# One split of V per chunk, low parts placed over the moving rows of U, expert choices looked up among 16 per side, and more gather pairs issued beside the routing

## The chip, the cores and the metric

The kernel runs on one core of one Trainium2 chip. The time is device microseconds of one execution, the median of several runs; the profiles show one execution each. Engines are called as in the profile: PE (TensorE matmul) and PEld (its weight loads), DVE (VectorE), ACT (ScalarE), POOL (GpSimd), SP (SyncE, which here only issues DMAs).

## What is computed

The program is one forward pass over 512 tokens of width 1024: a first block (neighbourhood attention beside a recurrent mixer, then a PEER feed-forward part), and a second block of two ordinary layers. The change touches the PEER part alone. Cut to that:

```python
def peer_ffn(h, wq, sub_keys, u, v):        # h 512 x 1024, u and v 16384 x 1024
    def block(t):                            # 128 tokens at a time
        q = (t @ wq).reshape(128, 8, 2, 128)
        s = jnp.einsum('tpcd,pckd->tpck', q, sub_keys)
        s1, i1 = lax.top_k(s[:, :, 0], 16)   # best 16 of 128 keys, each side
        s2, i2 = lax.top_k(s[:, :, 1], 16)
        cand = (s1[..., :, None] + s2[..., None, :]).reshape(128, 8, 256)
        cidx = (i1[..., :, None] * 128 + i2[..., None, :]).reshape(128, 8, 256)
        top, pos = lax.top_k(cand, 16)       # best 16 of the 256 sums
        idx = jnp.take_along_axis(cidx, pos, axis=-1)
        g = jax.nn.softmax(top, axis=-1)
        a = jax.nn.gelu(jnp.einsum('tpkd,td->tpk', u[idx], t), approximate=False)
        return jnp.einsum('tpk,tpkd->td', g * a, v[idx])
```

Each token has 8 heads with 16 chosen experts: 128 rows of u and 128 rows of v per token.

## The kernel before

All products are in fp32, made of three matmuls of a reduced-precision fp32 type: each operand is split into a high part (a copy by ACT) and a low part (operand minus high part, by DVE), and high x high, high x low and low x high are added up in PSUM.

**PEER, two ways at once.** Token tile 0 (128 tokens) goes by *gathers*: for each of its 128 (head, rank) places an indirect DMA on POOL's queue fetches 128 rows of U (one for each token, 512 KB), and DVE takes the dot product with the token (L1161, tile `gr`); later an indirect DMA fetches the rows of V, and DVE adds them weighted to `accg` (L1166). That is 256 gathers in 128 pairs (`gathered`, L1130). Five buffers `gr` form a ring, and a gather is issued four places ahead of the DVE operation that consumes it. Token tiles 1 to 3 (384 tokens) go *densely*: all 16384 experts are computed in 128 chunks of 128, and a weight table W with zeros for the experts that a token has not chosen is multiplied in.

**The U stage.** `ahead` (L1368) runs over the 128 chunks. `rows_u` loads 512 KB of U and splits it (`wh` on ACT L1349, `wl` on DVE L1350); `hidden` makes 24 matmuls of 128x384 and a gelu, and the result `act` goes to DRAM (`Ad`). Beside it `route` works through the tiles: `topk` (DVE alone) finds the experts of a tile, and `spread` turns them into the table W by one-hot matmuls: for each group of four tokens DVE makes `oh` and `go` (L1321), ACT scales `go`, PE multiplies, ACT copies the bank, and W goes to DRAM (`Wd`). The list `GATHER` gives for each of five phases (phase t runs topk of tile t beside spread of tile t-1) what a gather pair costs in the planner `weave`, which always takes the next piece of the generator that has spent least; a smaller number issues pairs more often. `PACE` (2.66) is the price of a chunk there. PE's order is the written one. The ring of gathers starts in phase 1, after the choices of tile 0 are known.

**The V stage.** After the last chunk of U, `operands` (L1377) prepares one chunk of V: it loads `act` and V, multiplies `act` by the weights `Wr` (L1390), and splits V and act. The split of V is written twice: `vh` (L1391, ACT) and `vl` (L1393, DVE), and again in the last line by the helper `split` (L134 on ACT, L136 on DVE); only the second pair is used. `products` makes 18 matmuls of 128x512 per chunk, four chunks behind. The gathers that are left are spread evenly over the first 120 chunks. The order on PE, DVE and ACT is the written one. The pools on the right side of SBUF are a stack: `h2` (the moving rows of U, the tokens) is closed after the last chunk of U, and `pm` (act, Wr, vh, vl, sh, sl) is opened in its place.

**The tail.** The six PSUM banks and `accg` are scaled by a row `gt2r`, added to X, normed (L1084 to L1104), and the second block begins. Line numbers from L1054 on are one to twelve different in the changed kernel; the order fences below show both.

Of the kernel before, what the change touches and what calls it, by code (L numbers as in the profile page):

```python
# [22 lines left out]
TD = S - T0  # L23
# [5 lines left out]
VBUFS = 6  # L29
# [2 lines left out]
WT = 16  # L32
GBUFS = 5
GAHEAD = 4
GATHER = (13.0, 13.0, 9.0, 6.0, 4.5)
OPS_LAG = 4
TAIL = 2
STATE = 3.0
# [54 lines left out]
class Net:  # L93
# [931 lines left out]
    def peer(self):  # L1025
        nc, p = self.nc, self.p
# [15 lines left out]
        pq = self.pool("pq", "right")  # L1042
# [9 lines left out]
        run(ahead)  # L1052
        self.shut("pa")
        self.shut("h2")  # L1054
        pm = self.pool("pm", "right")
        ar = self.pool("ar")
        for i in range(GROUP - WLATE):
            self.spread_rows(pm, 0, i)
        rows = self.rows_of(3, "gt2r", ar)
        banks = [[self.bank() for _ in range(2)] for _ in range(3)]  # L1060
        ops = {}
        held = []
# [2 lines left out]
        E = mybir.EngineType  # L1065
        with self.tc.manual_schedule(engines={E.PE, E.DVE, E.Activation}):
            for e in range(128 + OPS_LAG):
# [6 lines left out]
                if e >= OPS_LAG:  # L1074
                    x = e - OPS_LAG
                    if x < 128 - TAIL:
                        self.products(banks, range(3), [(x, ops.pop(x))])
                    else:
                        held.append((x, ops.pop(x)))
        run(gather)  # L1080
        for t in range(3):
            self.products(banks, [t], held)
        self.shut("pm")
# [160 lines left out]
    def topk(self, pq, sc, io):  # L1244
        nc = self.nc
        m1 = pq.tile([128, 8, 2, 16], F32, name="m1")
        i1 = pq.tile([128, 8, 2, 16], U32, name="i1")
        for h in range(8):
            for c in range(2):
                tmp = pq.tile([128, 128], F32, name="tmp", bufs=2)  # L1250
                self.top16(m1[:, h, c], i1[:, h, c], sc[:, h * 2 + c], tmp)
                yield 1.0
        f1 = pq.tile([128, 8, 2, 16], F32, name="f1")
        nc.vector.tensor_copy(f1, i1)
        nc.vector.tensor_scalar(f1[:, :, 0], f1[:, :, 0], 128.0, None, op0=OP.mult)
        cand = pq.tile([128, 8, 50], F32, name="cand")
        cidx = pq.tile([128, 8, 50], F32, name="cidx")
        for dst, src in ((cand, m1), (cidx, f1)):
            o = 0
            for a in range(8):  # L1260
                n = 16 // (a + 1)
                nc.vector.tensor_tensor(out=dst[:, :, o:o + n], in0=src[:, :, 0, a:a + 1].to_broadcast([128, 8, n]),
                                        in1=src[:, :, 1, :n], op=OP.add)
                o += n
            nc.vector.tensor_tensor(out=dst[:, :, o:], in0=src[:, :, 0, 8:],
                                    in1=src[:, :, 1, 0:1].to_broadcast([128, 8, 8]), op=OP.add)
        yield 2.7
        top = pq.tile([128, 8, 16], F32, name="top")
        pos = pq.tile([128, 8, 16], U32, name="pos")
        for h in range(8):  # L1270
            tmp = pq.tile([128, 128], F32, name="tmp", bufs=2)
            self.top16(top[:, h], pos[:, h], cand[:, h], tmp[:, :50])
            yield 0.6
        pf = pq.tile([128, 8, 16], F32, name="pf")
        nc.vector.tensor_copy(pf, pos)
        idx = pq.tile([128, 128], F32, name="idx", bufs=2)
        for h in range(8):
            eq = pq.tile([128, 16, 50], F32, name="eq")
            nc.vector.tensor_tensor(out=eq, in0=io[:, None, :50].to_broadcast([128, 16, 50]),
                                    in1=pf[:, h].unsqueeze(2).to_broadcast([128, 16, 50]), op=OP.is_equal)  # L1280
            self.anchor = nc.vector.tensor_tensor(out=eq, in0=eq, in1=cidx[:, h:h + 1].to_broadcast([128, 16, 50]), op=OP.mult)
            nc.vector.tensor_reduce(idx[:, h * 16:(h + 1) * 16], eq, axis=AX.X, op=OP.add)
            yield 2.7
        ii = pq.tile([128, 128], I32, name="ii")
        nc.vector.tensor_copy(ii, idx)
        e1 = pq.tile([128, 128], F32, name="e1", bufs=2)
        e2 = pq.tile([128, 128], F32, name="e2", bufs=2)
        it = pq.tile([128, 128], I32, name="it", bufs=2)
        nc.vector.tensor_scalar(it, ii, 7, None, op0=OP.logical_shift_right)
        nc.vector.tensor_copy(e1, it)  # L1290
        it = pq.tile([128, 128], I32, name="it", bufs=2)
        nc.vector.tensor_scalar(it, ii, 127, None, op0=OP.bitwise_and)
        nc.vector.tensor_copy(e2, it)
# [8 lines left out]
        return e1, e2, g.rearrange("p h k -> p (h k)")  # L1302

    def spread(self, pq, t, e1, e2, g, io):

# [71 lines left out]
    def operands(self, pm, e):  # L1377

        nc, p = self.nc, self.p
        n, j = divmod(e, GROUP)  # L1380
        if j == 0:
            self.Wr = self.Wn
        a = pm.tile([128, TD], F32, name="act", bufs=ABUFS)
        nc.sync.dma_start(a, self.Ad[e])
        v = self.st.tile([128, 2, 512], F32, name="w", bufs=WBUFS)
        nc.sync.dma_start(v.rearrange("p a b -> p (a b)"), p['V'][e])
        vh, vl = (pm.tile([128, 2, 512], FR, name=n, bufs=VBUFS) for n in ("vh", "vl"))
        sh, sl = (pm.tile([128, TD], FR, name=n, bufs=VBUFS) for n in ("sh", "sl"))
# [472 lines left out]
```

## Time and profile before

| | us |
|---|---|
| median of 3 runs | 3129.43 |
| lowest and highest run | 3128.04, 3133.86 |
| the profiled execution | 3129.33 |
| its span | 3127.5 |

| engine | busy us | share | 
|---|---|---|
| PE | 2937.5 | 94% |
| PEld | 2488.1 | 80% |
| DVE | 2033.6 | 65% |
| ACT | 1387.3 | 44% |
| POOL | 458.0 | 15% |

The span is one program of many stages; a share over the whole of it says little about any of them. The stages of this case are told apart by time: the U stage from 678.27 (its first matmul) to 1338.12 (the start of its last), and the V stage from 1349.76 to 1986.64. Busy time of PE is modelled, and matmuls overlap in the records: the distance between starts is the price of one, not its length. The same holds for DVE, where an operation's record is about 0.08 us longer than the distance to the next start.

### The profile page before, as it was taken

The numbers are of one execution on the slowest core, as the hardware profiler recorded it, in microseconds if no ns is written. First come the engines' busy times: TensorE is split into PE (matmuls) and PEld (weight loads), VectorE is DVE, ScalarE is ACT, GpSimd is POOL, SyncE is SP. The second block draws the span as 40 slices with busy tenths as digits, with TensorE's granted clock in tenths as the row PEclk, the third lists the DMA queues.
The fourth block names the chain that finished last, engine by engine and source line by source line (L and its number), as shares of the span: only waits on it lengthen the run. The fifth ranks groups of instructions, "written<-read, shape, count | busy, mean of one in ns | idle before, by whom it ended". The sixth has DMA issues, their size and how long they took to land.

```text
span 3127.5 us, 42558 instructions
## 1 busy us (share of the span) xinstructions
PE 2937.5 (94%) x16010; PEld 2488.1 (80%) x16010; DVE 2033.6 (65%) x3768; ACT 1387.3 (44%) x2404; POOL 458.0 (15%) x399
## 2 busy tenths in 40 slices
PE   7898998999999999978888888899999999999998
PEld 5787987899998999966666666678888887788887
DVE  5744496459999867679999999644433335543323
ACT  4233563343466667844444444533322234433222
POOL 2100000000111222224444443000000000000000
PEclk9999999999999999999999999899999999999999
DMA  6622202345666778899999998222333222123332
GB/s 251 226 69 78 62 1 95 108 133 193 225 231 218 267 263 290 294 311 337 342 338 337 341 341 306 87 71 90 101 99 97 95 88 66 51 88 96 100 102 81
DMA packets 262510, 544.63 MB, mean 174 GB/s; under 512 B 21904, under 2 KB 139936, under 8 KB 257952
## 3 DMA queue, kind: packets, MB, share of 16 engines
q1 hardware_dynamic: 200096, 350.28, 34.1%
q0 software_dynamic: 36896, 134.25, 12.6%
q10 hardware_dynamic: 25312, 57.39, 5.0%
q8 instruction: 125, 2.05, 0.3%
q14 instruction: 81, 0.66, 0.1%
HBM read 489.38 MB, written 52.45 MB: 173 GB/s over the span
## 4 chain that ended last, share of the span: by engine, by line
PE 53%; DVE 23%; issue 10%; DMA 2%; POOL 1%; ACT 1%; SPq 0%; POOLq 0%; ACTq 0%; DVEq 0%
PE bank L123 51%; DVE vl L1393 4%; DVE accg L1166 3%; DVE gr L1161 3%; DVE act L1390 2%; DVE sl L1394 2%; DVE wl L1350 1%; POOL gr L1142 1%; PE bank L608 1%; PE bank L1500 1%; DVE A L826 1%; DVE KX L802 1%; DVE QX L803 0%; DMA gr<-in_Un_dram,iu 0%; DVE tmp L1240 0%
## 5 line engine op out<-in xcount | busy, mean ns | idle before, releaser
L123 PE MATMUL bank<-hh,wl 128*128 128x512 f32 (+2 forms) x2304 | 837.0, 364 | 31.7 <-DVE wl L1350 21.2
L123 PE MATMUL bank<-hh,wh 128*128 128x512 f32 (+2 forms) x2304 | 840.5, 366 | 10.8 <-ACT wh L149 4.4
L123 PE MATMUL bank<-hl,wh 128*128 128x512 f32 (+2 forms) x2304 | 834.8, 362 | 1.8 <-DVE hl L273 1.1
L150 DVE TENSOR_TENSOR wl<-w,wh 128x1024 fp32r<-128x1024 f32 (+2 forms) x280 | 295.2, 1055 | 645.9 <-ACT wh L149 639.0
L149 ACT ACTIVATE wh<-w 128x1024 fp32r<-128x1024 f32 (+2 forms) x280 | 257.4, 920 | 746.1 <-PE bank L123 602.9
L123 PEld LDWEIGHTS bank<-hh,wl 128*128 128x128 f32 x2304 | 437.8, 190 | 89.9 <-DVE wl L1350 32.3
L123 PEld LDWEIGHTS bank<-hh,wh 128*128 128x128 f32 x2304 | 436.7, 190 | 64.8 <-ACT wh L149 5.0
L123 PEld LDWEIGHTS bank<-hl,wh 128*128 128x128 f32 x2304 | 437.8, 190 | 49.2 <-DVE hl L273 1.9
L1142 POOL DMA_INDIRECT gr<-in_V_dram,iv x128 | 212.4, 1660 | 588.1 <-DVE gr L1161 546.2
L123 PE MATMUL bank<-vl,sh 128*128 128x512 f32 x768 | 247.7, 404 | 42.9 <-DVE vl L136 42.8
L123 PE MATMUL bank<-vh,sh 128*128 128x512 f32 x768 | 245.4, 401 | 36.9 <-ACT vh L134 36.9
L123 PE MATMUL bank<-vh,sl 128*128 128x512 f32 x768 | 237.9, 391 | 0.0
L123 PEld LDWEIGHTS bank<-vl,sh 128*128 128x128 f32 x768 | 137.6, 188 | 105.7 <-DVE vl L136 82.0
L123 PEld LDWEIGHTS bank<-vh,sh 128*128 128x128 f32 x768 | 139.6, 188 | 89.8 <-ACT vh L134 63.5
L1142 POOL DMA_INDIRECT gr<-in_Un_dram,iu x128 | 165.9, 1296 | 295.1 <-DVE gr L1161 158.3
L1392 ACT ACTIVATE sh<-act 128x384 fp32r<-128x384 f32 x128 | 67.3, 526 | 309.1 <-DVE act L1390 309.1
L1349 ACT ACTIVATE wh<-w 128x1024 fp32r<-128x1024 f32 x128 | 135.4, 1058 | 142.3 <-PE bank L123 133.4
L1350 DVE TENSOR_TENSOR wl<-w,wh 128x1024 fp32r<-128x1024 f32 x128 | 156.1, 1220 | 62.1 <-ACT wh L1349 62.1
L123 PEld LDWEIGHTS bank<-vh,sl 128*128 128x128 f32 x768 | 144.5, 188 | 31.3
L217 POOL TENSOR_TENSOR r<-r,mhalf 128x1 f32<-128x1 f32 x37 | 21.7, 590 | 987.2 <-DVE r L216 979.8
L1161 DVE SCALAR_TENSOR_TENSOR gr<-gr,h 128x1024 f32<-128x1024 f32 x128 | 155.9, 1219 | 15.4 <-DMA gr<-in_Un_dram,iu 15.4
L1166 DVE SCALAR_TENSOR_TENSOR accg<-gr,wt,accg 128x1024 f32<-128x1024 f32 x127 | 162.7, 1281 | 0.4
(369 smaller groups left out, 5059.2 us busy)
## 6 DMA issues: line engine op xcount, KB each, us to landing
w<-in_U_dram SPq DMA_DIRECT2D x128, 512.0 KB
w<-in_V_dram SPq DMA_DIRECT2D x128, 512.0 KB
w<-in_wgu_dram SPq DMA_DIRECT2D x84, 512.0 KB
Ad<-act ACTq DMA_DIRECT2D x128, 192.0 KB
Wd<-W ACTq DMA_DIRECT2D x24, 1024.0 KB
Wr<-Wd SPq DMA_DIRECT2D x96, 256.0 KB
act<-Ad SPq DMA_DIRECT2D x128, 192.0 KB
w<-in_wdown_dram SPq DMA_DIRECT2D x44, 512.0 KB
```

The source lines that it names most:

```text
L123: return self.nc.tensor.matmul(out, a, b, start=start, stop=stop)
L149: self.nc.scalar.activation(hi[:, :, :n], w[:, :, :n], AF.Copy)
L150: (self.low or self.nc.vector).tensor_tensor(out=lo[:, :, :n], in0=w[:, :, :n], in1=hi[:, :, :n], op=OP.subtract)
L1142: nc.gpsimd.indirect_dma_start(out=t, out_offset=None, in_=table, in_offset=bass.IndirectOffsetOnAxis(ap=idx, axis=0))
L1161: nc.vector.scalar_tensor_tensor(t, t, 1.0, self.h0, op0=OP.mult, op1=OP.mult, accum_out=dots[:, h, k:k + 1])
L1166: nc.vector.scalar_tensor_tensor(acc, t, wt[:, h, k:k + 1], acc, op0=OP.mult, op1=OP.add)
L1349: nc.scalar.activation(uh, w, AF.Copy)
L1350: nc.vector.tensor_tensor(out=ul, in0=w, in1=uh, op=OP.subtract)
L1390: self.anchor = nc.vector.tensor_tensor(out=a3, in0=a3, in1=self.Wr[:, :, e % GROUP], op=OP.mult)
L1392: nc.scalar.activation(sh, a, AF.Copy)
L1393: nc.vector.tensor_tensor(out=vl, in0=v, in1=vh, op=OP.subtract)
L1394: nc.vector.tensor_tensor(out=sl, in0=a, in1=sh, op=OP.subtract)
```

## The change

- `operands` no longer calls `split`; the pair of L1391 and L1393 is used.
- A second pool, `pl`, is opened on the right ahead of `pm`, so it lies where `h2` was. The low parts `vl` and `sl` live in it. `pm` then lies further along.
- The row `gt2r` and its pool `ar` are created after the V loop instead of ahead of it.
- `topk`: the table of candidate sums has 80 columns in place of 50, built by 3 adds (9 before), and there is no table of expert numbers (9 adds before). A new function `ranks` turns a position in the table into the ranks on the two sides by 10 small operations, and each side's key number is looked up among 16 (4 times 3 operations on 1024 elements per tile; before, 8 times 3 on 800). The conversion of an expert number into its two halves is gone.
- `GATHER` is 3.4 and 2.1 in its last two phases (6.0 and 4.5 before).

```diff
-GATHER = (13.0, 13.0, 9.0, 6.0, 4.5)
+GATHER = (13.0, 13.0, 9.0, 3.4, 2.1)
...
         self.shut("h2")
+        self.late = self.pool("pl", "right")
         pm = self.pool("pm", "right")
-        ar = self.pool("ar")
         for i in range(GROUP - WLATE):
             self.spread_rows(pm, 0, i)
-        rows = self.rows_of(3, "gt2r", ar)
...
         run(gather)
+        ar = self.pool("ar")
+        rows = self.rows_of(3, "gt2r", ar)
         for t in range(3):
             self.products(banks, [t], held)
...
-        cand = pq.tile([128, 8, 50], F32, name="cand")
-        cidx = pq.tile([128, 8, 50], F32, name="cidx")
-        for dst, src in ((cand, m1), (cidx, f1)):
-            o = 0
-            for a in range(8):
-                n = 16 // (a + 1)
-                nc.vector.tensor_tensor(out=dst[:, :, o:o + n], in0=src[:, :, 0, a:a + 1].to_broadcast([128, 8, n]),
-                                        in1=src[:, :, 1, :n], op=OP.add)
...
+        cand = pq.tile([128, 8, 80], F32, name="cand")
+        nc.vector.tensor_tensor(out=cand[:, :, :16], in0=m1[:, :, 0, 0:1].to_broadcast([128, 8, 16]), in1=m1[:, :, 1], op=OP.add)
+        nc.vector.tensor_tensor(out=cand[:, :, 16:72].rearrange("p h (a b) -> p h a b", a=7),
+                                in0=m1[:, :, 0, 1:8].unsqueeze(3).to_broadcast([128, 8, 7, 8]),
+                                in1=m1[:, :, 1, None, :8].to_broadcast([128, 8, 7, 8]), op=OP.add)
...
-        for h in range(8):
-            eq = pq.tile([128, 16, 50], F32, name="eq")
-            nc.vector.tensor_tensor(out=eq, in0=io[:, None, :50].to_broadcast([128, 16, 50]),
-                                    in1=pf[:, h].unsqueeze(2).to_broadcast([128, 16, 50]), op=OP.is_equal)
-            self.anchor = nc.vector.tensor_tensor(out=eq, in0=eq, in1=cidx[:, h:h + 1].to_broadcast([128, 16, 50]), op=OP.mult)
-            nc.vector.tensor_reduce(idx[:, h * 16:(h + 1) * 16], eq, axis=AX.X, op=OP.add)
-            yield 2.7
...
+        ab = self.ranks(pq, pos, cand)
+        E = pq.tile([128, 2, 8, 16], F32, name="E", bufs=2)
+        for h in range(0, 8, 4):
+            hs = slice(h, h + 4)
+            for c in range(2):
+                eq = pq.tile([128, 4, 16, 16], F32, name="eq")
+                nc.vector.tensor_tensor(out=eq, in0=io[:, None, None, :16].to_broadcast([128, 4, 16, 16]),
+                                        in1=ab[c][:, hs].unsqueeze(3).to_broadcast([128, 4, 16, 16]), op=OP.is_equal)
+                self.anchor = nc.vector.tensor_tensor(out=eq, in0=eq, op=OP.mult,
+                                                      in1=f1[:, hs, c].unsqueeze(2).to_broadcast([128, 4, 16, 16]))
+                nc.vector.tensor_reduce(E[:, c, hs], eq, axis=AX.X, op=OP.add)
+                yield 3.4
...
+    def ranks(self, pq, pos, room):
...
+        for x, s, op in ((row, 3, OP.logical_shift_right), (low, 7, OP.bitwise_and)):
+            i = pq.tile([128, 8, 16], U32, name="ri")
+            nc.vector.tensor_scalar(i, pos, s, None, op0=op)
+            nc.vector.tensor_copy(x, i)
+        nc.vector.scalar_tensor_tensor(t, row, 9.0, low, op0=OP.is_ge, op1=OP.mult)
...
-        vh, vl = (pm.tile([128, 2, 512], FR, name=n, bufs=VBUFS) for n in ("vh", "vl"))
-        sh, sl = (pm.tile([128, TD], FR, name=n, bufs=VBUFS) for n in ("sh", "sl"))
+        vh, vl = (x.tile([128, 2, 512], FR, name=n, bufs=VBUFS) for x, n in ((pm, "vh"), (self.late, "vl")))
+        sh, sl = (x.tile([128, TD], FR, name=n, bufs=VBUFS) for x, n in ((pm, "sh"), (self.late, "sl")))
...
-        vh, vl = self.split(pm, v, [128, 2, 512], "v", bufs=TAIL + OPS_LAG)
```

**DVE in the middle of the V stage**, before and then after (`act`, `vl`, `sl` are a chunk's operands, `gr` and `accg` a gather pair):

```order
L1390 TENSOR_TENSOR act<-act,Wr 128x384
L1393 TENSOR_TENSOR vl<-w,vh 128x1024
L1394 TENSOR_TENSOR sl<-act,sh 128x384
L136 TENSOR_TENSOR vl<-w,vh 128x1024
L1161 SCALAR_TENSOR_TENSOR gr,dots<-gr,h_5502 128x1024
L1166 SCALAR_TENSOR_TENSOR accg<-gr,wt,accg 128x1024
L1390 TENSOR_TENSOR act<-act,Wr 128x384
```

```order
L1396 TENSOR_TENSOR act<-act,Wr 128x384
L1399 TENSOR_TENSOR vl<-w,vh 128x1024
L1400 TENSOR_TENSOR sl<-act,sh 128x384
L1396 TENSOR_TENSOR act<-act,Wr 128x384
L1399 TENSOR_TENSOR vl<-w,vh 128x1024
L1400 TENSOR_TENSOR sl<-act,sh 128x384
L1163 SCALAR_TENSOR_TENSOR gr,dots<-gr,h_5502 128x1024
L1168 SCALAR_TENSOR_TENSOR accg<-gr,wt,accg 128x1024
```

The operation of the helper (L136) is gone from each chunk, and a gather pair stands in about every second chunk. Over the whole stage DVE has 134 gather operations in place of 172.

**DVE late in the U stage**, in the last phase, where the table of tile 3 is made (`oh` and `go` are the one-hot tiles, `wl` a chunk's low part), before and then after:

```order
L1350 TENSOR_TENSOR wl<-w,wh 128x1024
L1321 TENSOR_TENSOR oh<-io,eT 128x512
L1321 TENSOR_TENSOR go<-io,eT 128x512
L1161 SCALAR_TENSOR_TENSOR gr,dots<-gr,h_5502 128x1024
L1166 SCALAR_TENSOR_TENSOR accg<-gr,wt,accg 128x1024
L1321 TENSOR_TENSOR oh<-io,eT 128x512
L1321 TENSOR_TENSOR go<-io,eT 128x512
L1350 TENSOR_TENSOR wl<-w,wh 128x1024
L1321 TENSOR_TENSOR oh<-io,eT 128x512
L1350 TENSOR_TENSOR wl<-w,wh 128x1024
L1321 TENSOR_TENSOR go<-io,eT 128x512
L1350 TENSOR_TENSOR wl<-w,wh 128x1024
```

```order
L1356 TENSOR_TENSOR wl<-w,wh 128x1024
L1168 SCALAR_TENSOR_TENSOR accg<-gr,wt,accg 128x1024
L1327 TENSOR_TENSOR oh<-io,eT 128x512
L1327 TENSOR_TENSOR go<-io,eT 128x512
L1163 SCALAR_TENSOR_TENSOR gr,dots<-gr,h_5502 128x1024
L1168 SCALAR_TENSOR_TENSOR accg<-gr,wt,accg 128x1024
L1327 TENSOR_TENSOR oh<-io,eT 128x512
L1327 TENSOR_TENSOR go<-io,eT 128x512
L1327 TENSOR_TENSOR oh<-io,eT 128x512
L1356 TENSOR_TENSOR wl<-w,wh 128x1024
L1327 TENSOR_TENSOR go<-io,eT 128x512
L1163 SCALAR_TENSOR_TENSOR gr,dots<-gr,h_5502 128x1024
```

Gather operations stand two or three to a chunk. Over the U stage DVE has 107 of them in place of 72. On PE the last one-hot matmul stands after chunk 111 (after chunk 124 before), and 17 chunks follow with nothing between them.

**SP where U ends and V begins**, before and then after (with the waits as the program sets them; the number behind an engine's name says nothing here):

```order
L1386 DMA w<-in_V_dram 128x1024 [waits DMAHW7_49,DMAHW6_49,DVE_49]
L1406 DMA Wr<-Wd 128x4x128 [waits DMAHW1_49,PE_49]
L1406 DMA Wr<-Wd 128x4x128 [waits DMAHW2_49]
L1406 DMA Wr<-Wd 128x4x128 [waits DMAHW4_49]
L1406 DMA Wr<-Wd 128x4x128 [waits DMAHW5_49]
L1406 DMA Wr<-Wd 128x4x128 [waits DMAHW6_49]
L1406 DMA Wr<-Wd 128x4x128 [waits DMAHW7_49,DMAHW3_49]
L371 DMA gt2r<-Rd 128x1024 [waits DMAHW3_49,DMAHW0_49,Activation_49]
L1384 DMA act<-Ad 128x384 [waits DMAHW1_49,PE_49]
```

```order
L1352 DMA w<-in_U_dram 128x1024 [waits DMAHW7_49,DMAHW0_49,DVE_49]
L1411 DMA Wr<-Wd 128x4x128 [waits DMAHW3_49,PE_49]
L1411 DMA Wr<-Wd 128x4x128 [waits DMAHW4_49]
L1352 DMA w<-in_U_dram 128x1024 [waits DMAHW5_49,DMAHW1_49,DVE_49]
L1411 DMA Wr<-Wd 128x4x128 [waits DMAHW6_49]
L1411 DMA Wr<-Wd 128x4x128 [waits DMAHW0_49]
L1352 DMA w<-in_U_dram 128x1024 [waits DMAHW1_49,DVE_49]
L1411 DMA Wr<-Wd 128x4x128 [waits DMAHW2_49]
L1411 DMA Wr<-Wd 128x4x128 [waits DMAHW3_49]
L1390 DMA act<-Ad 128x384 [waits DMAHW5_49,PE_49]
```

The loads of `Wr` and the first loads of `act` stand among the last 14 loads of U, and wait for PE's last one-hot matmuls and transposes in place of the last matmul of the U stage.

## Rows read from the trace of the kernel before

**Rows 1.** Page, the chain that ended last, shares by line.

```profile
PE bank L123 51%; DVE vl L1393 4%; DVE accg L1166 3%; DVE gr L1161 3%; DVE act L1390 2%; DVE sl L1394 2%; DVE wl L1350 1%; POOL gr L1142 1%; PE bank L608 1%; PE bank L1500 1%; DVE A L826 1%; DVE KX L802 1%; DVE QX L803 0%; DMA gr<-in_Un_dram,iu 0%; DVE tmp L1240 0%
```

**Rows 2.** PE's timeline where U begins and ends: start, length, operation, [idle before, releaser].

```profile
678.27 0.42 PE L123 MATMUL bank<-hh,wh 128*128 128x384 f32 x1
...
1338.12 0.34 PE L123 MATMUL bank<-hh,wl 128*128 128x384 f32 x1
1349.76 1.22 PE L123 MATMUL bank<-vh,sh 128*128 128x512 f32 x2 [11.30 <-ACT vh L134]
```

**Rows 3.** DVE's timeline where V ends, the first step of the tail.

```profile
1986.61 0.69 DVE L1096 TENSOR_TENSOR y<-accg,gt2r 128x512 f32<-128x512 f32 x1 [6.59 <-PE bank L123]
```

**Rows 4.** V stage: PE, PEld, DVE, ACT, POOL busy (count), PEclk, DMA share, GB/s.

```profile
1360.00:1940.00 580.00, 514.26 (x2082) 379.12 (x2081) 578.09 (x722) 281.08 (x352) 257.09 (x173) 1.00 0.98 340
```

**Rows 5.** DVE's timeline, one chunk of the V stage with a gather pair.

```profile
1701.21 1.22 DVE L1161 SCALAR_TENSOR_TENSOR gr<-gr,h 128x1024 f32<-128x1024 f32 x1
...
1702.35 1.28 DVE L1166 SCALAR_TENSOR_TENSOR accg<-gr,wt,accg 128x1024 f32<-128x1024 f32 x1
1703.55 0.55 DVE L1390 TENSOR_TENSOR act<-act,Wr 128x384 f32<-128x384 f32 x1
1704.02 1.22 DVE L1393 TENSOR_TENSOR vl<-w,vh 128x1024 fp32r<-128x1024 f32 x1
1705.16 0.55 DVE L1394 TENSOR_TENSOR sl<-act,sh 128x384 fp32r<-128x384 f32 x1
1705.64 1.23 DVE L136 TENSOR_TENSOR vl<-w,vh 128x1024 fp32r<-128x1024 f32 x1
1706.78 1.22 DVE L1161 SCALAR_TENSOR_TENSOR gr<-gr,h 128x1024 f32<-128x1024 f32 x1
```

**Rows 6.** Waits from 1350 to 1986: who for whom, total us, times, longest.

```profile
ACT sh L1392 <- DVE act L1390: 300.8, 126, 3.3
...
PE bank L123 <- DVE vl L136: 42.8, 89, 0.5
```

**Rows 7.** Chain through a later feed-forward stage: start, us, what.

```profile
2198.32 355.86 PE bank L123 x1582
```

**Rows 8.** DMA from 1360 to 1940: rate in 40 slices of 14.5 us.

```profile
GB/s 318 302 378 344 310 383 296 343 382 295 350 358 313 376 347 291 382 320 340 385 289 349 361 298 367 358 300 382 322 333 376 266 368 388 288 366 368 274 379 340
```

**Rows 9.** DVE's timeline where V begins.

```profile
1347.64 0.56 DVE L1390 TENSOR_TENSOR act<-act,Wr 128x384 f32<-128x384 f32 x1 [15.32 <-DMA act<-Ad]
```

**Rows 10.** SP's issues where U ends.

```profile
1332.77 4.53 SPq L1406 DMA_DIRECT2D Wr<-Wd  x6
```

**Rows 11.** Chain in the U stage: start, us, what.

```profile
788.75 54.00 PE bank L123 x310
```

**Rows 12.** PE's timeline around two groups of one-hot matmuls.

```profile
1134.73 1.95 PE L123 MATMUL bank<-go,oh 128*128 128x128 f32 x16
1136.44 0.42 PE L123 MATMUL bank<-hh,wh 128*128 128x384 f32 x1
```

**Rows 13.** Waits from 662 to 1340, as in Rows 6.

```profile
PE bank L123 <- DVE wl L1350: 21.2, 24, 2.7
...
DVE gr L1161 <- DMA gr<-in_Un_dram,iu: 15.4, 5, 6.1
```

**Rows 14.** Groups from 662 to 1340: count, busy us, mean ns, idle before.

```profile
L1350 DVE TENSOR_TENSOR wl<-w,wh 128x1024 fp32r<-128x1024 f32 x128 | 156.1, 1220 | 62.1 <-ACT wh L1349 62.1
...
L1279 DVE TENSOR_TENSOR eq<-io,pf 128x800 f32<-128x800 f32 x32 | 31.6, 986 | 0.2
```

**Rows 15.** DVE's timeline late in the U stage.

```profile
1079.77 1.22 DVE L1161 SCALAR_TENSOR_TENSOR gr<-gr,h 128x1024 f32<-128x1024 f32 x1 [6.06 <-DMA gr<-in_Un_dram,iu]
...
1082.06 0.68 DVE L1321 TENSOR_TENSOR oh<-io,eT 128x512 f32<-128x512 f32 x1
1082.66 0.69 DVE L1321 TENSOR_TENSOR go<-io,eT 128x512 f32<-128x512 f32 x1
...
1091.48 1.23 DVE L1161 SCALAR_TENSOR_TENSOR gr<-gr,h 128x1024 f32<-128x1024 f32 x1 [3.45 <-DMA gr<-in_Un_dram,iu]
```

More of the change, by code (lines that the diff above doesn't have):

```diff
@@ L1080, in peer @@
         run(gather)
+        ar = self.pool("ar")
+        rows = self.rows_of(3, "gt2r", ar)
         for t in range(3):
             self.products(banks, [t], held)
-        self.shut("pm")
+        for name in ("pm", "pl"):
+            self.shut(name)
         pt = self.xp = self.pool("pt", "right")
@@ L1254, in topk @@
         nc.vector.tensor_copy(f1, i1)
-        nc.vector.tensor_scalar(f1[:, :, 0], f1[:, :, 0], 128.0, None, op0=OP.mult)
-        cand = pq.tile([128, 8, 50], F32, name="cand")
-        cidx = pq.tile([128, 8, 50], F32, name="cidx")
-        for dst, src in ((cand, m1), (cidx, f1)):
-            o = 0
-            for a in range(8):
-                n = 16 // (a + 1)
-                nc.vector.tensor_tensor(out=dst[:, :, o:o + n], in0=src[:, :, 0, a:a + 1].to_broadcast([128, 8, n]),
-                                        in1=src[:, :, 1, :n], op=OP.add)
-                o += n
-            nc.vector.tensor_tensor(out=dst[:, :, o:], in0=src[:, :, 0, 8:],
-                                    in1=src[:, :, 1, 0:1].to_broadcast([128, 8, 8]), op=OP.add)
-        yield 2.7
+        cand = pq.tile([128, 8, 80], F32, name="cand")
[3 more added lines that the diff above has]
+                                in1=m1[:, :, 1, None, :8].to_broadcast([128, 8, 7, 8]), op=OP.add)
+        nc.vector.tensor_tensor(out=cand[:, :, 72:], in0=m1[:, :, 0, 8:],
+                                in1=m1[:, :, 1, 0:1].to_broadcast([128, 8, 8]), op=OP.add)
+        yield 1.2
         top = pq.tile([128, 8, 16], F32, name="top")
@@ L1271, in topk @@
             tmp = pq.tile([128, 128], F32, name="tmp", bufs=2)
[L1272 to L1276, printed above, removed]
-        for h in range(8):
-            eq = pq.tile([128, 16, 50], F32, name="eq")
-            nc.vector.tensor_tensor(out=eq, in0=io[:, None, :50].to_broadcast([128, 16, 50]),
-                                    in1=pf[:, h].unsqueeze(2).to_broadcast([128, 16, 50]), op=OP.is_equal)
-            self.anchor = nc.vector.tensor_tensor(out=eq, in0=eq, in1=cidx[:, h:h + 1].to_broadcast([128, 16, 50]), op=OP.mult)
-            nc.vector.tensor_reduce(idx[:, h * 16:(h + 1) * 16], eq, axis=AX.X, op=OP.add)
-            yield 2.7
@@ L1284, in topk @@
[L1284 to L1292, printed above, removed]
@@ L1293, in topk @@
-        nc.vector.tensor_copy(e2, it)
+            self.top16(top[:, h], pos[:, h], cand[:, h], tmp[:, :80])
+            yield 0.7
+        ab = self.ranks(pq, pos, cand)
[10 more added lines that the diff above has]
+                yield 3.4
@@ L1294, in topk @@
+        e1, e2 = (E[:, c].rearrange("p h k -> p (h k)") for c in range(2))
         g = pq.tile([128, 8, 16], F32, name="g", bufs=2)
@@ L1302, in topk @@
         return e1, e2, g.rearrange("p h k -> p (h k)")
+    def ranks(self, pq, pos, room):
+        nc = self.nc
+        row, low, a, t = (room[:, :, i * 16:i * 16 + 16] for i in range(4))
+        for x, s, op in ((row, 3, OP.logical_shift_right), (low, 7, OP.bitwise_and)):
[3 more added lines that the diff above has]
+        nc.vector.scalar_tensor_tensor(t, row, 9.0, low, op0=OP.is_ge, op1=OP.mult)
+        nc.vector.tensor_scalar(a, row, -1.0, 0.0, op0=OP.add, op1=OP.max)
+        nc.vector.tensor_tensor(out=a, in0=a, in1=t, op=OP.add)
+        nc.vector.tensor_tensor(out=low, in0=low, in1=t, op=OP.subtract)
+        nc.vector.tensor_scalar(row, row, 1.0, 8.0, op0=OP.is_equal, op1=OP.mult)
+        nc.vector.tensor_tensor(out=row, in0=row, in1=low, op=OP.add)
+        return a, row
     def spread(self, pq, t, e1, e2, g, io):
```

## Prediction

> **What bounds the kernel now.** The page comes first: its chain that ended last goes half by PE's one matmul line, and then by DVE lines that all belong to the V stage, `vl`, `accg`, `gr`, `act`, `sl` [rows 1]. So two stages have to be looked at by themselves. PE's timeline cuts them: the U stage runs from 678.27 to 1338.3 (660 us), the V stage from 1349.76 [rows 2] to 1986.6, where the tail takes over [rows 3]: 636.8 us, with a gap of 11.3 us ahead of it.
>
> In the V stage the window view shows DVE busy 578 of 580 us, PE's records 514 [rows 4]. DVE has no holes, and its timeline gives the price of each operation as the distance to the next start: dot 1.14, `accg` 1.20, `act` 0.47, `vl` 1.14, `sl` 0.48, the second `vl` 1.14; a chunk with a gather pair is 5.57 us [rows 5]. The list of waits says the same from the other side: ACT waits 126 times for `act`, and PE 89 times for the helper's `vl`, the very operation that is made a second time [rows 6]. How fast PE would go if nothing held it is read from a later feed-forward stage with matmuls of the same 128x512: 355.86 / 1582 = 0.225 us [rows 7], so 18 of them make 4.05 us per chunk and 128 chunks 518 us. The third resource there is the DMA: its engines show a share of 0.98 and 340 GB/s [rows 4], though DVE was what the gathers waited for; slices swing between 266 and 388 [rows 8].
>
> In the U stage PE leads: an undisturbed stretch takes 54.00 / 310 = 0.174 us per matmul [rows 11], so 128 x 24 make 535 us; two groups of one-hot matmuls take 1.71 us [rows 12], so 96 groups make 82. That is 617 of 660: PE stands still for about 43 us. 21.2 of it are put down to `wl` by name, and DVE itself waited 15.4 us for gathers, in five waits [rows 13].
>
> **The V stage, part by part.** Each chunk loses one DVE operation of 1.14 us (128 x 1.14 = 146 us of DVE) and one copy on ACT, which was not the limit. The order has 134 gather operations there in place of 172: 63 dots and 71 accumulations, 63 x 1.14 + 71 x 1.20 = 157 us; the chunk's own 0.47 + 1.14 + 0.48 = 2.09, times 128, is 268. DVE's sum is 425, under PE's 518: PE or DMA is next. DMA: a chunk loads 524 KB of V, 197 of act and 197 of Wr, 918 KB; some 130 gathers of 524 KB fall in the first 120 chunks, 568 KB per chunk, so 1.49 MB. If 340 GB/s at a share of 0.98 is the ceiling (347 at a share of 1), a chunk takes 4.28 us, 120 of them 514, and the last eight at PE's pace 32: 546. If the engines can carry what the best slices show, 388, a chunk takes 3.83, under PE's 4.05, and the stage is 518. The rows lean to neither: the mean was taken while DVE set the pace, and the slices are short. I take 535, some way to the upper end because packets of two queues will collide as now. Gain 637 - 535 = **102** (91 to 119).
>
> The Trainium skill, "DMA: Bandwidth & Descriptors", section "Where 436 GB/s comes from", says that between HBM and SBUF the HBM side binds at about 358 GB/s per core, and not the fabric's 435. By that rule a chunk of 1.49 MB would take 4.15 us and the stage 530, an estimate from that page, 5 us less than my value; the slices of 376 to 388 GB/s [rows 8] speak against it as a strict ceiling.
>
> **The gap between the stages.** Now the loads of `Wr` go out at 1332.77 [rows 10], those of act behind them, because their place was held by the moving rows until PE's last U matmul; DVE waits 15.3 us for them [rows 9], and ACT's and DVE's first splits follow. In the changed order these loads wait for the last one-hot matmul and the writes of W, 16 chunks (some 67 us) ahead of the end, and the first multiplication by `Wr` stands between the low parts of U chunks 115 and 116. Only `vl` and `sl` wait for the last U matmul, which is one 1.14 us operation ahead of the second matmul of V. Gap 11.3 to about 1.2: gain **10**. What is queued behind the moved waits: SP's last 11 loads of U and DVE's low parts from 116 on. The cover is about three chunks, 12 us, of prefetched U; if the W writes come later than that, DVE stops there for the 4 or 5 us that such a load takes now; I keep 0 to 5 us in the range.
>
> **The U stage.** Removed on DVE: lookups, 32 x 3 operations of 0.986 us = 95 [rows 14] (the other two operations taken at the price of the first); added, 16 x 3 on 1024 elements in place of 800, 1.26 us each = 61; 32 lists of 80 columns in place of 50, 5 operations each, 30 x 1.23 ns = 6 more. Small operations (adds, conversions, `ranks`) come and go in similar number, counted at nothing, at most a few us either way. Net -28. Added: 35 gather operations, 41 us. So DVE has 13 us more to do in a stage of which 43 us were already lost. What decides is where. The planner finishes the routing earlier: the last one-hot matmul stands after chunk 111 and no longer after 124, so the work that had 37 chunks of cover is pressed together, and DVE does almost nothing in the last 17 chunks, 71 us. In that last stretch (chunks 95 to 111) the order has about 1.9 groups of `oh` and `go` at 2 x 0.60 us [rows 15], 2.5 gather operations and one `wl` per chunk: 2.3 + 2.9 + 1.14 = 6.35 us of DVE against 24 x 0.174 + 1.9 x 0.855 = 5.8 of PE. Running the two orders through with these prices, and nothing else, PE stands 21 us before and 39 after: +18. The 22 us that this sum misses of the 43 are largely late gathers; with 107 gathers for 72 the 15.4 become 23: +7. I take **+25**. Low end: -5, if the lookups' saving in the DVE-bound first phases counts in full and the late stretch stays covered; high end +60, below.
>
> **The tail.** The first step of the tail now waits for PE's very last matmul [rows 3]. In the changed order it waits for the one 38 matmuls earlier, 38 x 0.225 = 8.6 us, and tile by tile after that; what remains behind the last bank is one tile's work. I take **-6** (0 to -8).
>
> **Sum.** The profiled execution is 3129.3 us, and the median of three 3129.4, so nothing is to be converted: 3129.3 - 102 - 10 + 25 - 6 = **3036**.
>
> **The rivals.** *All covers hold*: V at PE's 518, the U stage +8. 3129.3 - 119 - 10 + 8 - 6 = 3002. For it: the slices near 388; against it: two collisions would both have to stay away.
>
> *The gain is eaten in part by late gathers*: the ring has five buffers, a pair is now asked for every 4 to 5 us in the last two phases, and DVE, whose order is fixed, holds the next `wl` behind each late one, as at 1079.77 (6.06 us) and 1091.48 (3.45) [rows 15]. If 15 of the added ones wait the mean of now, 15.4 / 5 = 3.1 us, the U stage is at +25 + 46, part of it on slack: +60; with V at 546: 3129.3 - 91 - 10 + 60 - 6 = 3082.
>
> *Slower*: the same mechanism without bounds. All the 80 or so gather operations of the two last phases stand late and each holds DVE, then PE. The net gain without late gathers is 102 + 10 + 6 - 18 = 100, so it turns at 1.25 us per operation; at 3.1 us it is 248 and the time 3129.3 - 100 + 248 = 3277. Against it: five waits in 72 now, and a late gather lets the following ones arrive.
>
> *The change does not free the V stage*, because the DMA is what held it all along: then 117 MB of chunk loads and 68 of gathers at 340 GB/s still give 546, for there are fewer gathers in it. That is inside the range, at about 3047; a V stage of 620 or more would need a wait that no row shows.
>
> **How the numbers follow.** Forecast with V from 522 to 546 and U from +12 to +40: 0.57, by itself 3015 to 3062. All covers hold: 0.18. Late gathers eat a part: 0.2. Slower: 0.03; within 0.2% (about what a measurement of this kernel can tell from no change): 0.02. The range reaches from the second case's 3002 to the third's 3082, where about 0.15 is left out on both sides.
>
> **What would show it.** Right: DVE well under full in the V stage (some 68%), PE's first operand waits there gone or put down to DMA, matmul starts 0.225 to 0.24 us apart; the gap around 1 us; no U matmul waiting after chunk 112; DVE's waits for `gr` in the U stage at 20 to 40 us. Wrong: DVE waits for `gr` of 100 us and more, or PE waiting for act and V loads in the V stage with the DMA share at 1 (then DMA, not PE, sets 546 or more), or a stop of DVE between low parts 115 and 116.

## The result and the profile after

The changed kernel takes 3025.1 us (median of four runs, 3021.7 to 3029.2) where the kernel before takes 3130.9: a ratio of 0.966 (0.965 to 0.968). The forecast was 3036. The profiled execution of the changed kernel is 3021.7 us, 107.7 less than that of before. Cut at the same places, by the starts of matmuls (the V stage ends, and the tail begins, with the last two matmuls, which the timeline shows as one row at 1986.41 and 1886.37; the very last one starts at 1986.64 and 1886.60):

| part | before | after | change | forecast |
|---|---|---|---|---|
| U stage | 659.8 | 684.4 | +24.5 | +25 |
| gap to the first V matmul | 11.6 | 0.2 | -11.5 | -10 |
| V stage | 636.7 | 523.0 | -113.7 | -102 |
| tail, to the first 256-column matmul | 18.8 | 11.7 | -7.1 | -6 |
| all | | | -107.7 | -93 |

The page's chain by line, as in [rows 1]:

```profile
PE bank L123 64%; POOL gr L1144 2%; DMA gr<-in_Un_dram,iu 1%; DVE wl L1356 1%; PE bank L608 1%; PE bank L1505 1%; DVE accg L1168 1%; DMA gr<-in_V_dram,iv 1%; DVE KX L802 1%; DVE A L826 1%; DVE QX L803 0%; DVE gr L1163 0%; DVE tmp L1242 0%; DVE go L1327 0%; DVE oh L1327 0%
```

The DVE lines of the V stage have nearly left the chain. The V stage by window (columns as in [rows 4]) and the chain through it (start, us, what):

```profile
1375.00:1860.00 485.00, 485.00 (x2141) 401.61 (x2140) 420.71 (x573) 183.11 (x248) 199.20 (x135) 1.00 1.04 376
```

```profile
1364.89 516.45 PE bank L123 x2277
```

PE has no hole in 485 us and its matmuls follow at 516.45 / 2277 = 0.227 us. DVE is busy 87%, and the DMA carries 376 GB/s at a share of 1.04 (this share is a sum of the times of packets and can pass 1). By the trace DVE has 142 gather operations in the stage (180 before), and 114 in the U stage (76 before). Where U ends, PE's and then DVE's timeline, as in [rows 2] and [rows 3]:

```profile
1363.23 0.34 PE L123 MATMUL bank<-hh,wl 128*128 128x384 f32 x1
1363.41 0.63 PE L123 MATMUL bank<-vh,sh 128*128 128x512 f32 x2
1364.89 0.73 PE L123 MATMUL bank<-vl,sh 128*128 128x512 f32 x2 [0.85 <-DVE vl L1399]
```

```profile
1878.41 1.29 DVE L1098 TENSOR_TENSOR y<-accg,gt2r 128x512 f32<-128x512 f32 x2 [11.30 <-PE bank L123]
```

V's first matmul follows U's last without a break; what is left of the gap is the 0.85 us that PE waits for the first `vl`. The tail's first step starts at 1878.4, 8 us ahead of V's last matmul (1886.6). What became worse is the U stage. Its waits, as in [rows 13]:

```profile
PE bank L123 <- DVE wl L1356: 33.7, 32, 4.3
DVE gr L1163 <- DMA gr<-in_Un_dram,iu: 28.6, 10, 6.6
```

Both are larger than before (21.2 and 15.4). Another wait stands late in the stage: DVE, between the low parts of chunks 115 and 116, waits for the first load of `act`, and PE then for the next low part.

```profile
1311.98 0.56 DVE L1396 TENSOR_TENSOR act<-act,Wr 128x384 f32<-128x384 f32 x1 [6.49 <-DMA act<-Ad]
```

```profile
1313.72 0.45 PE L123 MATMUL bank<-hh,wl 128*128 128x384 f32 x1 [1.75 <-DVE wl L1356]
```

### The profile page after: what moved, and what is told of

It reads as the page before. It is cut to its first block, busy times and chain, and to the rows that moved or that the text cites. A ratio compares the mean times of both kernels' runs of the same rounds, so it can differ in the third digit from the quotient of the medians.

```text
span 3019.9 us, 42272 instructions
## 1 busy us (share of the span) xinstructions
PE 2901.4 (96%) x16010; PEld 2505.5 (83%) x16010; DVE 1856.1 (61%) x3544; ACT 1269.6 (42%) x2276; POOL 448.6 (15%) x399
## 4 chain that ended last, share of the span: by engine, by line
PE 66%; issue 9%; DVE 9%; DMA 3%; POOL 2%; ACT 1%; POOLq 0%; SPq 0%; ACTq 0%; DVEq 0%
PE bank L123 64%; POOL gr L1144 2%; DMA gr<-in_Un_dram,iu 1%; DVE wl L1356 1%; PE bank L608 1%; PE bank L1505 1%; DVE accg L1168 1%; DMA gr<-in_V_dram,iv 1%; DVE KX L802 1%; DVE A L826 1%; DVE QX L803 0%; DVE gr L1163 0%; DVE tmp L1242 0%; DVE go L1327 0%; DVE oh L1327 0%
## 5 line engine op out<-in xcount | busy, mean ns | idle before, releaser
L1144 POOL DMA_INDIRECT gr<-in_V_dram,iv x128 | 204.6, 1598 | 455.7 <-DVE gr L1163 406.4
L123 PE MATMUL bank<-vl,sh 128*128 128x512 f32 x768 | 236.6, 389 | 0.9 <-DVE vl L1399 0.9
L123 PE MATMUL bank<-vh,sh 128*128 128x512 f32 x768 | 236.4, 389 | 0.0
L1399 DVE TENSOR_TENSOR vl<-w,vh 128x1024 fp32r<-128x1024 f32 x128 | 156.0, 1219 | 67.1 <-ACT vh L1397 59.1
L1397 ACT ACTIVATE vh<-w 128x1024 fp32r<-128x1024 f32 x128 | 134.9, 1054 | 134.2 <-DMA w<-in_V_dram 128.1
L1163 DVE SCALAR_TENSOR_TENSOR gr<-gr,h 128x1024 f32<-128x1024 f32 x128 | 155.8, 1219 | 28.8 <-DMA gr<-in_Un_dram,iu 28.6
L123 PEld LDWEIGHTS bank<-vl,sh 128*128 128x128 f32 x768 | 144.1, 188 | 31.2 <-DVE vl L1399 1.3
```

The source lines that it names most:

```text
L123: return self.nc.tensor.matmul(out, a, b, start=start, stop=stop)
L1144: nc.gpsimd.indirect_dma_start(out=t, out_offset=None, in_=table, in_offset=bass.IndirectOffsetOnAxis(ap=idx, axis=0))
L1163: nc.vector.scalar_tensor_tensor(t, t, 1.0, self.h0, op0=OP.mult, op1=OP.mult, accum_out=dots[:, h, k:k + 1])
```

## The experiments

### What the second split was worth

Put back into the changed kernel:

```diff
+        vh, vl = (x.tile([128, 2, 512], FR, name=n, bufs=VBUFS) for x, n in ((pm, "vh"), (self.late, "vl")))
+        nc.scalar.activation(vh, v, AF.Copy)
+        nc.vector.tensor_tensor(out=vl, in0=v, in1=vh, op=OP.subtract)
         return sh, sl, vh, vl
```

> The changed kernel, with the second split of V put back (one more copy on ACT and one more 1.14 us subtraction on DVE in each of 128 chunks; the second pair is used, as before). Theory (the V stage was held by DVE, and the second split was what held it): DVE's sum in the V stage goes from 425 to 571 us, over PE's 518, so the stage takes 575 or so where the changed kernel takes 523, and the time is about 3025 + 50 = 3075. Rival (the gain of the V stage came from fewer gathers in it, DVE has room): the stage stays at 523 to 530, the time at 3025 to 3032.

Measured: 3098.5 us, ratio to the kernel before 0.989 (0.987 to 0.991); the V stage takes 593.2 us, U and gap are as in the changed kernel (683.7 and 0.2), and the tail is 17.4 in place of 11.7. The window 1380 to 1860 and a line of the waits from 1370 to 1880:

```profile
1380.00:1860.00 480.00, 447.81 (x1869) 344.14 (x1869) 478.87 (x602) 251.46 (x315) 183.49 (x124) 1.00 0.97 332
```

```profile
PE bank L123 <- DVE vl L1405: 26.3, 62, 0.5
```

DVE is full again and PE waits for the second `vl` by name. So the split is worth 70 us of the V stage here, and 73 in the medians with the 6 us of the tail. The other way round, the kernel before with that one line removed:

```diff
-        vh, vl = self.split(pm, v, [128, 2, 512], "v", bufs=TAIL + OPS_LAG)
         return sh, sl, vh, vl
```

> The kernel before, with nothing changed but that V is split once. 172 gather operations stay in the V stage: DVE's sum is 470 us, under PE's 518; the DMA has to move 207 MB in it. Theory that the DMA engines carry about 376 GB/s at most, as in the changed kernel's V stage: 551 us, time 3130 - 86 = 3044. Theory that they still have room there: 523 to 530, time 3016 to 3023, no slower than the whole change. Theory of a ceiling at 347 (340 at a share of 0.98, in the kernel before): 597, time 3090.

Measured: 3068.0 us, 0.979 (0.978 to 0.981); the V stage takes 571.7 us, more than any of the sums that took DVE or PE for the limit. The DMA carried 377 GB/s at a share of 1.04 from 1380 to 1860, while PE had holes (columns as in [rows 4]):

```profile
1380.00:1860.00 480.00, 458.56 (x1922) 354.12 (x1921) 409.70 (x559) 160.64 (x217) 224.24 (x158) 0.99 1.04 377
```

That is 65 us under the kernel before (3133.2 beside this run), of the 106 of the whole change; the rest has to come from the other parts.

### Which resource sets the V stage once DVE is free

The changed kernel with the gather prices of before:

```diff
-GATHER = (13.0, 13.0, 9.0, 3.4, 2.1)
+GATHER = (13.0, 13.0, 9.0, 6.0, 4.5)
```

> The changed kernel with the two gather prices of before (6.0 and 4.5). 35 gather operations go back from the U stage to the V stage. Theory (the U stage pays for the added gathers, 25 us longer than before because of them): the U stage shrinks from 685 to 650 to 660, and DVE's waits for gathers there from 29 us to about 15. The V stage then has 172 gather operations and takes 523 if the DMA has room, 551 if 376 GB/s is the ceiling: 2995 to 3025 in all. Rival (the U stage is longer because the routing is pressed into fewer chunks, not because of gathers): U stage 675 to 685, time 3020 to 3050.

Measured: 3044.9 us, 0.972 (0.970 to 0.974). The U stage shrinks to 662.4 and DVE's waits for gathers to 5.4 us, as the theory had it, but the V stage grows to 566.8. By the counts in the traces 44 gather operations went over and not 35 (186 in the V stage where the changed kernel has 142). The window 1380 to 1860, and PE's longest wait from 1342 to 1905:

```profile
1380.00:1860.00 480.00, 459.48 (x1928) 354.65 (x1927) 419.72 (x569) 161.79 (x218) 234.98 (x167) 0.99 1.05 385
```

```profile
PE bank L123 <- ACT sh L1398: 18.6, 15, 3.1
```

PE has holes again, DVE is at 87%, and PE waits for `sh`, which ACT makes. ACT's `vh` waits 142.7 us for the loads of V, but it waits 127.3 in the changed kernel too, where PE has no hole, so the list of waits does not settle it. To see whether it is the bytes, the same kernel without most loads of `Wr` (the weights of the chunks from the third group on are left out of the calculation):

```diff
+        if n > 1:
+            return
         if i == 0:
             self.Wn = pm.tile([128, TD // WT, GROUP, WT], F32, name="Wr", bufs=2)
```

> The changed kernel with the gather prices of before (as in the run with 567 us in the V stage), in which Wr is loaded for the first two groups of eight chunks alone and used again for the others (the weights of the later chunks are left out). That takes 197 KB per chunk, a seventh of the bytes, off the DMA, and nothing off any engine. Theory (567 us was the DMA's time): the V stage falls to 523 to 530. Rival (it was DVE's or the ring's, with 44 more gather operations): it stays at 560 or more.

Measured: the V stage takes 523.0 us with all 186 gather operations in it, the whole 3001.9 us.

```profile
1380.00:1860.00 480.00, 480.00 (x2119) 397.48 (x2118) 453.85 (x615) 179.36 (x246) 249.17 (x169) 1.00 0.96 364
```

By the traces a tenth of the bytes is gone from the stage (22 of 210 MB, not the seventh that was expected) and with them 44 of 108 thousand packets, and PE has no hole, though DVE is busier than in the changed kernel (454 of 480). So it was the DMA; whether bytes or packets count, this run does not part. Together with the two runs in which PE had holes it gives the ceiling for this mix of loads: 377 to 385 GB/s, held over 480 us. The move of 44 gather operations into the U stage is worth 44 us in the V stage and costs 22 in the U stage: 20 us in the medians. (The change itself moves 38, from 76 to 114.)

### The place of the low parts

```diff
-        vh, vl = (... for x, n in ((pm, "vh"), (self.late, "vl")))
-        sh, sl = (... for x, n in ((pm, "sh"), (self.late, "sl")))
+        vh, vl = (... for x, n in ((pm, "vh"), (pm, "vl")))
+        sh, sl = (... for x, n in ((pm, "sh"), (pm, "sl")))
```

> The changed kernel with vl and sl back in the one pool pm, which then lies where the moving rows of U were. Theory (the place in SBUF alone closes the gap between the stages): the gap of 1 us is 11 again, time 3025 + 10 = 3035. Rival (the loads come early for another reason, such as the end of the routing): no difference, 3025.

Measured: 3036.8 us, 0.969 (0.968 to 0.971), 12 us more than the changed kernel. PE's timeline where V begins, then DVE's at the tail:

```profile
1369.76 1.22 PE L123 MATMUL bank<-vh,sh 128*128 128x512 f32 x2 [6.79 <-ACT sh L1398]
```

```profile
1894.67 0.69 DVE L1098 TENSOR_TENSOR y<-accg,gt2r 128x512 f32<-128x512 f32 x1 [18.63 <-PE bank L123]
```

The gap is 7.1 us, and the tail is 18.8 us as before the change: the second half of its first step starts with V's last matmul (1894.7) again. So the second pool is worth 7 us at either place. The tail's buffers (`y`) are opened where the last closed pool lay: over `vl` and `sl`, where the wait ends with a matmul 38 ahead of the end, or over `pm`, where it ends with the third from last. The other 4.5 us of the gap have no run of their own. In the trace before, the first load of `act` goes out at 1343.26, 5.1 us after the start of U's last matmul and right behind `gt2r` on SP (1342.83), whose load the change moves to the end of the V stage; in this run it goes out 2.7 us after that matmul. The kernel before with one split has a gap of 10.7.

### Why the U stage became longer

Five ways of taking the pressure off were tried first. The choices of before in the changed kernel (`topk` as it stood, and `GATHER` at 3.7 and 2.2 so that the number of gathers in the stage is nearly the same):

> The changed kernel with the choices of before (50 candidates with their expert numbers, 8 times 3 operations on 800 elements per tile), and the last two gather prices at 3.7 and 2.2, so that nearly the same number of gather operations stands in the U stage (two more). About 28 us of DVE work come back into the U stage. Theory (DVE leads where the routing stands, and what the lookups saved has paid for part of the gathers): the U stage goes from 684 to 700 to 712, the V stage stays at 523, time 3040 to 3053. Rival (the lookups saved nothing that counts, since with the old gather prices the U stage is 662 with the new choices and 660 with the old): the U stage stays at 680 to 690, time 3020 to 3030.

Measured: 3018.7 us, 0.963 (0.962 to 0.965), U stage 680.5. The rival holds: the interval overlaps that of the changed kernel (0.965 to 0.968), so the new lookups are not shown to gain or to lose anything. They are cheaper on DVE (the three operations take 58.4 us in the trace after, 94.4 before), but DVE's time was not what the stage lacked.

One more buffer in the ring:

```diff
-GBUFS = 5
-GAHEAD = 4
+GBUFS = 6
+GAHEAD = 5
...
```

> The changed kernel with six gather buffers in place of five, and gathers issued five places ahead in place of four (the ring in a pool of its own, two small tiles shared to make room). Theory (the U stage loses its 22 to 25 us to gathers that land late: DVE waits 28.6 us for them, in ten waits): these waits fall under 15 us and the U stage from 684 to 665 to 672, time 3005 to 3013. Rival (it is the 41 us of gather work itself, too much for DVE in the last two phases): waits fall but the U stage stays at 680 or more, time 3020 to 3026.

Measured: 3021.7 us, 0.965 (0.964 to 0.967); DVE's waits for gathers fall from 28.6 to 20.0 us only, the U stage to 679.2. Not to be told from the changed kernel.

Eight pairs behind the routing, where DVE has little to do:

```diff
-GATHER = (13.0, 13.0, 9.0, 3.4, 2.1)
+GATHER = (13.0, 13.0, 9.0, 3.4, 2.6)
+SPARE = 8
...
         while self.routing:
             yield next(gather)
             n += 1
+        for _ in range(SPARE):
+            yield (next(gather), 2 * PACE)[1]
+            n += 1
...
```

Behind the routing these gather operations are then placed after the low parts of U (the lines that do so are left out above).

> The changed kernel with fewer pairs beside the last phase of the routing (price 2.6 for 2.1) and eight pairs in the 17 chunks of U behind it, one for every two chunks, where DVE has a single low part per chunk to make. Eight gather operations fewer stand in the V stage. Theory (what costs is the crowding on DVE before chunk 112, and the chunks behind it have room): the U stage 684 becomes 670 to 678, the V stage stays at 523, time 3010 to 3019. Rival (the U stage loses its time earlier, in phases 2 and 3, which this leaves alone): the U stage stays at 682 or more, time 3021 to 3026.

> Both together: six gather buffers, and eight pairs moved behind the routing. If lateness and crowding are two causes, the gains add up: U stage 655 to 665, time 2995 to 3006. If they are the same loss seen twice, the time is that of the better one of the two alone.

Measured: 3026.8 us (0.966, 0.964 to 0.968) for the first and 3024.4 us (0.965, 0.964 to 0.967) for both together, U stages 685.5 and 685.4. No gain is shown by either.

The routing stretched again to chunk 124:

```diff
-PACE = 2.66
+PACE = 2.38
```

> The changed kernel with a chunk of U priced at 2.38 in place of 2.66 in the planner, so that the routing ends after chunk 124, as before the change, and not after 111; the numbers of gather operations in both stages are the same. Theory (the U stage loses time because the routing with its gathers is pressed into 111 chunks): U stage 684 becomes 665 to 675, time 3006 to 3016. Rival (the loss goes by DVE's work, wherever it stands): 680 to 686, time 3021 to 3027; the last loads of Wr and act then come later, and the gap of 0.2 us may open by 2 to 5.

Measured: 3024.9 us, 0.967 (0.965 to 0.968), U stage 684.1, and the gap opens to 2.8 us. DVE's waits for gathers come to 39.1 us in this stage, 10.5 more than in the changed kernel, and the stage is not longer for it. So it is not that the routing is pressed into fewer chunks.

That left DVE's work against the gathers' supply. First DVE's work cut to a quarter of the columns with the bytes left as they are (both lines of a gather's arithmetic work on `[:, :256]`):

```diff
-nc.vector.scalar_tensor_tensor(t, t, 1.0, self.h0, ...)
+nc.vector.scalar_tensor_tensor(t[:, :256], t[:, :256], 1.0, self.h0[:, :256], ...)
```

> The changed kernel in which the DVE operation of a gather works on 256 of the 1024 columns (dot and accumulation alike; the rest of tile 0's sums is left out). The gathers, their number, order and bytes are the same; each costs DVE about 0.3 us in place of 1.14 to 1.20. Theory (in the U stage the added gathers cost by DVE's time, which holds the low parts): the U stage goes from 684 to 650 to 660, the V stage stays at 523, time about 2995. Rival (they cost by landing late and by the DMA): the U stage stays at 678 to 685, time 3018 to 3025.

Measured: 3016.1 us, 0.963 (0.961 to 0.965); the U stage takes 679.7, as the rival had it. A dot's record is 0.42 us and an accumulation's 0.48 (1.22 and 1.28 before), so DVE has some 85 us less to do in the stage and waits instead:

```profile
DVE gr L1163 <- DMA gr<-in_Un_dram,iu: 28.7, 13, 8.5
...
DVE accg L1168 <- DMA gr<-in_V_dram,iv: 12.5, 6, 3.4
```

Then the bytes cut to a quarter with DVE's work left as it is:

```diff
-nc.gpsimd.indirect_dma_start(out=t, out_offset=None, in_=table, ...)
+nc.gpsimd.indirect_dma_start(out=t[:, :256], out_offset=None, in_=table.rearrange("n (a c) -> (n a) c", c=256), ...)
...
+                t4 = t[:, None, :256].to_broadcast([128, 4, 256])
...
```

(The product of a dot is written over `accg` here, in place of `gr`.)

> The changed kernel in which each gather fetches 256 columns in place of 1024 (a quarter of the bytes, from other rows; tile 0's sums are wrong by that), while its DVE operation still works on 1024 elements, reading the 256 four times. It is the counterpart of the run in which the bytes stayed and DVE's work was cut to a quarter (U stage 680 in place of 684). Theory now, since that run spoke against DVE's work: the added gathers cost by their supply (bytes on a DMA that is full late in the stage, and landing late): DVE's waits for gathers of 28.6 us go to under 8, and the U stage from 684 to 660 to 668, time 3000 to 3009. Rival (both causes stand in for each other: with the one taken away, the other holds PE as long): the U stage stays at 676 to 684, time 3017 to 3025. The V stage stays at 523 with DMA share far under 1 in both.

Measured: 2995.3 us, 0.957 (0.955 to 0.959); the U stage takes 656.7 us, 3 us less than before the change, with all the added gather operations at full price on DVE (1.22 and 1.28). The waits from 662 to 1340 have no DVE wait for a gather any more; of PE:

```profile
PE bank L123 <- DVE wl L1358: 15.1, 21, 2.4
```

The stretch of the last routing phase, 1180 to 1280, in the changed kernel and in this run (columns as in [rows 4]):

```profile
1180.00:1280.00 100.00, 95.42 (x595) 91.71 (x595) 97.47 (x133) 79.73 (x171) 52.17 (x39) 0.98 0.99 372
```

```profile
1180.00:1280.00 100.00, 96.66 (x604) 93.13 (x603) 88.32 (x116) 76.48 (x157) 44.69 (x34) 1.00 0.75 254
```

With full gathers the DMA is at 372 GB/s there, near the ceiling that the V stage showed. The 27.7 us between 684.4 and 656.7 are those of the gathers' bytes and packets, of all 114 gather operations in the stage and not of the added ones alone. No run parts the late gathers themselves from other loads that they slow down, but the trace of the changed kernel speaks for the first. From 678 to 1300 it lists no wait of ACT or DVE for a load of U, and two of PE's four longest stops stand right behind a late gather, since DVE's order has the dot ahead of the next `wl`. DVE's timeline at one of them, then PE's:

```profile
1118.98 1.23 DVE L1163 SCALAR_TENSOR_TENSOR gr<-gr,h 128x1024 f32<-128x1024 f32 x1 [6.57 <-DMA gr<-in_Un_dram,iu]
...
1120.13 1.22 DVE L1356 TENSOR_TENSOR wl<-w,wh 128x1024 fp32r<-128x1024 f32 x1
```

```profile
1121.40 0.53 PE L123 MATMUL bank<-hh,wl 128*128 128x384 f32 x1 [3.22 <-DVE wl L1356]
```

What a late gather costs is not its wait, though: with the routing stretched, 39.1 us of waits went with the same 684.1. No run cut the bytes of the U stage alone; the V stage is 523.0 in both.

## Why the prediction was right, and where not

The time lies inside the range, 11 us under the forecast, and the direction and the order of the terms hold. By its steps:

**V stage: right in mechanism, the term too small by 12 us.** DVE was the limit and the second split was its load (the run with both splits). The choice between PE's 518 and the DMA's 546 was wrong: I took 535, the run shows 523.0, PE's pace (0.227 us per matmul in place of 0.225). The ceiling of 347 GB/s, read as 340 at a share of 0.98, was no ceiling: the same engines carry 376 at a share of 1.04 when DVE does not hold the gathers back. The best slices of [rows 8] were the better reading. I also counted eight gather operations too few in the stage, before and after (172 for 180, 134 for 142), and too few in the U stage (72 for 76, 107 for 114). The rule of the Trainium skill that I had weighed, "DMA: Bandwidth & Descriptors", section "Where 436 GB/s comes from", would have made an estimated 530 of it, with 358 GB/s; the trace does not agree, with 376 over 485 us.

**The DMA as the next limit: right, one step later.** It does not hold PE in the changed kernel but lies a little beyond: with 44 more gather operations it sets 567. The rate does not tell the two apart (376 GB/s here, 377 in the kernel before with one split, where PE had holes); the holes do. The single split by itself gave 65 us only, and without the move of gathers the change is 20 us slower. That the two belong together was not in the prediction, which counted the move as a cost in the U stage.

**Gap and tail: right in size** (10 and 6 forecast, 11.5 and 7.1 measured). For the tail the order showed the wait and not the reason; the run with the low parts in `pm` shows that it is the second pool. For the gap the reason was right in part: the second pool gives 7 of the 11.5, and the load of `gt2r`, ahead of those of `act` in SP's order, was not in the working. Nor did U's last matmul hold the loads of `Wr`: they went out at 1332.77 [rows 10], 5 us ahead of it (1338.12).

**U stage: the number right by luck, the reason wrong.** +25 was forecast and +24.5 measured, but the working was 18 us of DVE crowded before chunk 112 and 7 of late gathers. Stretching the routing to chunk 124, moving pairs behind it, and taking 85 us of the gathers' DVE work away changed the stage by 5 us at most; taking three quarters of the bytes away gave 27.7 back. The step that failed is the sum of DVE and PE per chunk, 6.35 against 5.8 us: it left out the third resource, though the same argument had been made for the V stage. The run with a quarter of the bytes has all of DVE's added work and a U stage 3 us shorter than before. The -28 us of lookups were real on DVE (-36 for the three operations), and no run shows a gain from them. DVE's stop between the low parts 115 and 116 came, 6.5 us, and cost PE 1.75, inside the 0 to 5 that were kept for it.

**The rivals.** That late gathers eat part of the gain is the mechanism that the runs and the trace speak for in the U stage, at about the price of the main forecast and not at +60. *All covers hold* had the better V stage (518 for 523) and the worse U stage (+8). The slower case stayed far off: ten waits of 2.9 us on average, not eighty.

**The signs.** Matmul starts (0.227 us), the gap and DVE's waits for `gr` (28.6 us) are as named. DVE's share is not: 87% in place of "some 68%". The 68 does not come out of the prediction's own sum either, for 425 of 535 us is 79%; with 0.08 us taken off each of the 573 records in the window, the measured share is an estimated 77%. And one U matmul waits after chunk 112 (at 1313.72, above).

## What to carry to other kernels

A share of 0.98 of the DMA engines beside an engine that is full says nothing yet on the DMA's ceiling: the short windows with the highest rate come closer than the mean. When one engine's work is removed, add up each resource for each stage again, bytes included, also in the stage to which work is moved. An edit that is cheaper on an engine (here the lookups) may be worth nothing where that engine's time is not what the stage lacks, and the memory under a pool can decide when the next stage may begin.

## What the runs showed of the hardware

A stop of PE can cost more than its length. The windows around the stop of 3.22 us shown above, which ends at 1121.40 (columns as in [rows 4]):

```profile
1118.00:1121.40 3.40, 0.18 (x2) 0.00 (x0) 2.42 (x4) 0.00 (x0) 0.92 (x1) 1.00 0.36 146
1121.40:1125.00 3.60, 3.60 (x12) 3.60 (x13) 2.50 (x4) 2.41 (x5) 0.76 (x1) 0.53 0.70 248
1125.00:1128.60 3.60, 3.60 (x22) 3.60 (x21) 3.56 (x6) 2.10 (x4) 1.10 (x1) 1.00 0.81 222
```

Behind the stop the granted clock is at half, the lower level of 1.2 GHz, and the matmuls follow at 0.32 us in place of 0.174 (12 of them in 3.60 us, then 22), until the clock rises again. A stop of 3.61 us that ends at 1090.30 is followed by the same. The longest stop, 4.30 us from 985.2, is not of this kind: the clock was at half as it began, behind a stop of 1.41 us that ended at 983.2, and stayed there until 995.3. Over the U stage 44 matmuls follow at 0.32, 6 us more than at full clock (before the change 19 and 3 us): of the 25 us by which the stage grew, some 4 are the clock's.

The DMA engines carried 376 to 385 GB/s over 480 us from two queues at once, at shares of 1.04 to 1.05, where one queue held the loads and the other the gathers.
